# Two transformer layers on one core: the issue order of TensorE and the places of the small matrix products

## Chip, core and metric

The kernel runs on one core of a Trainium2 chip. Time is device microseconds of one launch; lower is better. TensorE (PE) multiplies matrices and transposes, VectorE (DVE), ScalarE (ACT) and GpSimd (POOL) work elementwise, SyncE (SP) issues the transfers.

## The reference

A sequence of 256 rows of 1024 numbers passes through two layers. Each adds a token mixer and then an MLP to the residual `x`. Layer 0 mixes with differential attention, layer 1 with sparse attention, in which an indexer chooses 64 keys for each query. The queries of a chunk of 64 rows see the keys of their own and of earlier chunks.

```python
for i in range(2):
    h = rms_norm(x, norm_mix[i])
    if i == 0:   # 8 heads, two softmaxes each
        q, k, v = split(h @ w_in)                  # q, k: 16 x 64, RMS-normed, rotary
        a = softmax(q1 @ k1.T) - lam * softmax(q2 @ k2.T)
        mix = (rms_norm(a @ v) * (1 - lam_init)) @ w_out
    else:        # 16 heads of 64
        c_q, k, v, k_idx, w_idx = split(h @ w_in)
        q, q_idx = rms_norm(c_q) @ w_uq, rms_norm(c_q) @ w_uq_idx
        score = sum_h(w_idx[h] * relu(q_idx[h] @ k_idx.T))
        chosen = top_k(score, 64)                  # per query
        mix = (softmax(q @ k[chosen].T) @ v[chosen]) @ w_out
    x = x + mix
    u = relu(rms_norm(x, norm_mlp[i]) @ w1)        # 1024 -> 4096
    x = x + (u * u) @ w2
```

All of it is float32. The indexer's choice is made as a mask here: all keys stay, and those not chosen get a large number added.

## The kernel before

**Wide products.** The weights come in units of 128 x 2048 numbers, 1 MB each (`unit`). A unit is split in two parts of reduced width whose sum is the number: ACT writes the high part (`whi`, L160), DVE the rest (`wlo`, L161, mostly in two pieces of 128 x 1024). The activations are kept in the same two parts. One wide product of the mathematics is three on PE (`mm3`, L164 to L170): high times high (L165), high times low (L167), low times high (L169), each 128 x 512 in the output. In the first half of an MLP it is two instructions (L492, L495). PE runs some 1,500 of these.

**Small products.** Between them stand the products of the mixers and the transposes:

- `make_h` (L242) transposes the residual into the next layer's input; ACT and DVE write the two parts (L246, L248). It is called for each half (256 columns) of a 128 x 512 block of the residual as soon as DVE has summed that half (L472 in `out_proj`, L542 in `mlp`).
- `qk_post` norms and rotates queries and keys on DVE (L381, L388, `rope` L366 to L369), and transposes them on PE, four transposes for each of two halves `b` (L398).
- `scores` multiplies queries and keys (`dots`, L414) and adds the mask while taking the minimum on DVE (L425); `expo` makes the exponentials on ACT (L436) after a small scale on DVE (L434).
- In layer 0, `diff_probs` mixes the two softmaxes of a head on DVE (L629). `to_keys` transposes the result (L443, three transposes), `weighted` (L450 to L452) multiplies by the values, and `diff_out` norms that and transposes it (L658) for the output projection.
- In layer 1, `compress` transposes the compressed queries (L718), `index` projects and rotates the indexer's queries and keys, transposes them (L754, L767), scores (L414) and chooses: eight rounds of a maximum and a replacement for each of two row blocks on DVE (L792, L793). `dsa_probs` makes the probabilities of 8 heads, normalised at L839, and `dsa_out` multiplies by the values (L850, L851).

**What sets the order.** The mixers' parts are Python generators. `spawn` runs one up to its first `yield`; `tick`, after each wide product of `mm3`, counts the waiting ones down and lets one go on when its count is at zero; `need` runs one to its end. The count comes from the table `PAUSE` by the name of the stage, and is 0 for a name that isn't in it; the table holds eight names. That sets the source's order. The engines' queues, PE's too, are then put in order by the framework's scheduler, which takes the instructions by its own estimate of when their operands are there; so PE's queue is not the source's order. Each engine runs its own queue in order. Waits between engines go through semaphores.

**Buffers.** Three raw units (`wraw`), four split units (`wsp`), four PSUM banks for wide products (`acc`) and four for small ones (`wk`), six score tiles (`s`).

Of the kernel before, what the change touches and what calls it, by code (L numbers as in the profile page):

```python
# [44 lines left out]
PAUSE = {"idx scores 1": 1, "idx transposes 0": 1, "idx transposes 1": 36, "q1 transposes 0": 1,  # L45
         "out0": 1, "out1": 2, "out2": 24, "out3": 27}
# [3 lines left out]
def trunk(ctx: ExitStack, tc: tile.TileContext, x_in, first_in, pack_in, wf, out):  # L50
# [59 lines left out]
    def pause(stage):  # L110
        return PAUSE.get(stage, 0)
# [123 lines left out]
    def make_h(h, gc, t, n, js=(0, 1)):  # L235

        hi, lo, _ = h[n]
        for j in js:
            ps = wk()[:, :256]
            for i in range(2):  # L240
                c = n * 4 + j * 2 + i
                nc.tensor.transpose(ps[:, i * 128:(i + 1) * 128], x[t][:, c * 128:(c + 1) * 128], ident)  # L242
            ops = [((slice(None), j * 2 + i, slice(t * 128, t * 128 + 128)), ps[:, i * 128:(i + 1) * 128],
                    pack[:, gc + n * 4 + j * 2 + i:gc + n * 4 + j * 2 + i + 1]) for i in range(2)]
            for o, p, g in ops:
                behind[:] = [nc.scalar.activation(hi[o], p, AF.Copy, scale=g).ins]  # L246
            for o, p, g in ops:
                nc.vector.scalar_tensor_tensor(lo[o], p, g, hi[o].bitcast(F32), op0=OP.mult, op1=OP.subtract)  # L248

    def lhs(h, kt, t):  # L250
        hi, lo = h[kt // 4][:2]
        c = slice(t * 128, t * 128 + 128)
        return hi[:, kt % 4, c], lo[:, kt % 4, c]
# [117 lines left out]
    def qk_post(ps, m, scon, ty, ng, nq, gcols, nm):  # L371
# [19 lines left out]
        res = []  # L391
        for b in range(2):
            yield pause(f"{nm} transposes {b}")
# [60 lines left out]
    def out_proj(o, us, h, gc, needs=((),) * 4):  # L454
# [3 lines left out]
        for u, (wh, wl) in enumerate(us):  # L458
# [3 lines left out]
            for n in range(2):  # L462
                for t in range(2):
# [5 lines left out]
                    if u == 3:  # L469
                        for j in range(2):  # L470
# [3 lines left out]
                            make_h(h, gc, t, n, (j,))  # L474

    def mlp(h, after):
# [4 lines left out]
        def up(b):  # L481
# [5 lines left out]
            def group(ps, m, ks):  # L487

                wh, wl = w[m // 2]
                c = slice((m % 2) * 128, (m % 2) * 128 + 128)  # L490
                for k in ks:
                    mm(ps.rearrange("p (a b) -> p a b", b=256), wh[:, k, c], h[k // 4][2][:, :, k % 4],  # L492
                       start=k == 0, stop=False)
                for k in ks:
                    mm(ps[:, 256:], wl[:, k, c], h[k // 4][0][:, k % 4], start=False, stop=k == 7)  # L495

# [24 lines left out]
        for b in range(NB):  # L521
# [9 lines left out]
            for t, u, n in order:  # L531
# [7 lines left out]
                if last and u == 1:  # L539
                    for j in range(2):  # L540
# [3 lines left out]
                        after(t, n, j)  # L544
# [66 lines left out]
    def diff_probs(ps, res, nm):  # L611
# [4 lines left out]
        sts = []  # L616
        for hh in range(2):
            yield pause(f"{nm} scores {hh}")
            sts.append(scores(qT, kT, hh, cmask))
        for hh in range(2):  # L620
            z, st = zs[:, hh], sts[hh]
# [9 lines left out]
            yield pause(f"{nm} keys {hh}")  # L631
            aTs.append(to_keys(a))
        res += [aTs, zs]

    def diff_out(j, aTs, zs):
# [18 lines left out]
        yield pause(f"out{j}")  # L654
# [28 lines left out]
    for n in range(2):  # L683
        v_part(n, h, srow)
        for j in (2 * n, 2 * n + 1):
            need(probs[j])
            outs.append(spawn(diff_out(j, *pr[j])))
# [3 lines left out]
    mlp(h, lambda t, n, j: make_h(h1, C_NORM + 16, t, n, (j,)))  # L691
# [19 lines left out]

    def compress():
        craw = sc.tile([128, 2, 328], F32, name="qn")
        pt = wk()
        for t in range(2):
            nc.scalar.activation(craw[:, t], cps[t][:, :328], AF.Copy)
# [8 lines left out]
        return craw  # L725

    def index(craw):
# [20 lines left out]
        yield pause("idx queries")  # L748
        ps = [wk() for _ in range(2)]
# [46 lines left out]
    craw = compress()  # L796
    chosen = spawn(index(craw))
# [12 lines left out]
    uq = [a.rearrange("p (k n) -> p k n", n=D) for a in unit(pieces=2)]  # L810
    for n in range(2):
# [10 lines left out]
    def dsa_probs(half, out):  # L822
# [4 lines left out]
        st = {}  # L827
        for p in range(5):
            yield pause(f"probs {half}{p}")
            if p < 4:  # L830
# [157 lines left out]
```

## Time and profile before

| | us |
|---|---|
| median of three runs (604.1 to 606.72) | 604.16 |
| the profiled execution | 605.11 |
| its span, first to last instruction | 602.9 |
| PE busy | 590.3 |
| DVE busy | 429.8 |
| ACT busy | 366.0 |
| mean granted clock of TensorE, share of full | 0.995 |

The span has these stages, by the times of the trace: the differential attention up to about 119 us, of which the projections with scores and mixtures lie at 24 to 64 and on to 90; the first MLP to about 290; the sparse attention from there to about 417, its index scores at 322 to 326, its first normal scores at 359; and the second MLP. PE's instructions are pipelined: a wide product is shown as 0.39 long, but the next one starts 0.23 behind it, so places are read from start to start. In a line of the timeline, x6 means that six alike instructions in a row stand together.

### The profile page before, as it was taken

What the parts mean: (1) busy time and instruction counts of PE and PEld (TensorE: products, weight loads), DVE (VectorE), ACT (ScalarE), POOL (GpSimd) and SP (SyncE); (2) the same over time, 40 slices, a digit from 0 to 9 for tenths busy, and PEclk for the clock granted to TensorE, in tenths of its full rate; (3) what the DMA queues carried; (4) which work ended last, traced back from release to release, by engine and by line L of the source; (5) the groups of instructions that cost most, each with busy time, mean ns of one, the idle gap of its engine ahead of it and who ended that gap; (6) DMA issues with size and microseconds to landing.
All of it is one profiled execution on the core that took longest, in us unless ns stands there. A gap on an engine that the chain in (4) does not pass through costs nothing.

```text
span 602.9 us, 8418 instructions
## 1 busy us (share of the span) xinstructions
PE 590.3 (98%) x3052; PEld 487.7 (81%) x3052; DVE 429.8 (71%) x1060; ACT 366.0 (61%) x711; POOL 18.8 (3%) x53
## 2 busy tenths in 40 slices
PE   9999999999999999999999899999999999999997
PEld 7777777888888888888787687768888888888885
DVE  6799975688656656657598999766886576567542
ACT  5998987575545545535497489785855355445420
POOL 6500000000000000000000000000000000000000
PEclk9999999999999999999999899999999999999999
DMA  8856334336555445545364226323475456456401
GB/s 312 334 205 221 133 139 141 140 140 223 204 201 204 170 186 209 195 161 188 140 210 140 71 70 219 131 79 132 151 268 198 160 201 210 162 188 209 140 1 70
DMA packets 15449, 103.35 MB, mean 171 GB/s; under 512 B 1712, under 2 KB 1968, under 8 KB 3760
## 3 DMA queue, kind: packets, MB, share of 16 engines
q1 hardware_dynamic: 15408, 102.82, 48.3%
q8 instruction: 24, 0.39, 0.2%
q14 instruction: 17, 0.14, 0.1%
HBM read 101.76 MB, written 1.05 MB: 171 GB/s over the span
## 4 chain that ended last, share of the span: by engine, by line
PE 83%; DVE 10%; ACT 3%; DMA 2%; issue 1%; SPq 0%; DVEq 0%; ACTq 0%
PE wk L492 18%; PE acc L167 16%; PE acc L169 15%; PE acc L165 15%; PE wk L495 9%; DVE wlo L161 3%; DVE s L425 2%; PE wk L443 2%; PE acc L492 1%; PE wk L414 1%; PE wk L242 1%; DMA raw<-in_first 1%; DMA raw<-in_w 1%; PE wk L398 1%; DVE qkss L381 1%
## 5 line engine op out<-in xcount | busy, mean ns | idle before, releaser
L161 DVE TENSOR_TENSOR wlo<-raw,whi 128x1024 fp32r<-128x1024 f32 (+2 forms) x206 | 225.3, 1124 | 107.0 <-ACT whi L160 106.5
L160 ACT ACTIVATE whi<-raw 128x1024 fp32r<-128x1024 f32 (+2 forms) x206 | 193.3, 979 | 87.8 <-issue 46.2
L167 PE MATMUL acc<-wlo,act 128*128 128x512 f32 (+1 forms) x504 | 198.7, 394 | 1.0 <-DVE wlo L161 0.8
L169 PE MATMUL acc<-whi,act 128*128 128x512 f32 (+1 forms) x504 | 198.5, 394 | 0.0
L165 PE MATMUL acc<-whi,act 128*128 128x512 f32 (+1 forms) x504 | 197.7, 394 | 0.0
L492 PE MATMUL wk<-act,whi 128*128 128x512 f32 x480 | 120.6, 392 | 0.0
L167 PEld LDWEIGHTS acc<-wlo,act 128*128 128x128 f32 x504 | 95.5, 190 | 21.3 <-DVE wlo L161 1.8
L169 PEld LDWEIGHTS acc<-whi,act 128*128 128x128 f32 x504 | 95.4, 189 | 19.5 <-issue 1.7
L165 PEld LDWEIGHTS acc<-whi,act 128*128 128x128 f32 x504 | 95.3, 190 | 18.3 <-issue 0.7
L492 PEld LDWEIGHTS wk<-act,whi 128*128 128x128 f32 x480 | 86.8, 189 | 15.8
L495 PEld LDWEIGHTS wk<-act,wlo 128*128 128x128 f32 x480 | 66.0, 190 | 5.1
L495 PE MATMUL wk<-act,wlo 128*128 128x256 f32 x480 | 67.5, 282 | 0.0
L503 ACT ACTIVATE act<-on 128x256 fp32r<-128x256 f32 x64 | 26.4, 416 | 52.0 <-DVE on L502 51.9
L436 ACT ACTIVATE s<-s,nb,rs_r 128x128 f32<-128x128 f32 x64 | 34.2, 537 | 8.7 <-DVE nb L434 8.7
L500 ACT ACTIVATE sq<-wk 128x256 f32<-128x256 f32 x60 | 22.4, 374 | 28.1 <-PE wk L495 28.1
L504 DVE TENSOR_TENSOR act<-on,act 128x256 fp32r<-128x256 f32 x64 | 26.9, 423 | 14.6 <-ACT act L503 13.0
L502 DVE SCALAR_TENSOR_TENSOR on<-sq 128x256 f32<-128x256 f32 x64 | 27.0, 424 | 1.7
L501 DVE TENSOR_TENSOR sq<-wk,sq 128x256 f32<-128x256 f32 x60 | 25.1, 419 | 0.1
L246 ACT ACTIVATE act<-wk,pack 128x128 fp32r<-128x128 f32 x48 | 13.8, 378 | 8.0 <-PE wk L242 8.0
L542 DVE SCALAR_TENSOR_TENSOR x<-acc,rows,x 128x256 f32<-128x256 f32 x16 | 7.0, 479 | 15.7 <-PE acc L169 15.7
L443 PE MATMUL wk<-pack,s 128*128 128x128 f32 x72 | 15.5, 286 | 2.7 <-DVE s L629 1.9
L443 PEld LDWEIGHTS wk<-pack,s 128*128 128x128 f32 x72 | 8.9, 140 | 10.4 <-DVE s L629 4.2
(185 smaller groups left out, 441.2 us busy)
## 6 DMA issues: line engine op xcount, KB each, us to landing
raw<-in_w SPq DMA_DIRECT2D x91, 1024.0 KB, 4.8
raw<-in_w SPq DMA_DIRECT2D x2, 512.0 KB, 8.3
x<-in_x SPq DMA_DIRECT2D x2, 512.0 KB, 6.5
raw<-in_w SPq DMA_DIRECT2D x1, 984.0 KB, 4.7
raw<-in_w SPq DMA_DIRECT2D x1, 840.0 KB, 4.6
raw<-in_first SPq DMA_DIRECT2D x1, 768.0 KB, 5.8
out_dram<-x SPq DMA_DIRECT2D x3, 256.0 KB, 2.0
raw<-in_first SPq DMA_DIRECT2D x1, 512.0 KB, 6.7
```

Of the source, the lines that this page charges most:

```text
L160: split[:] = [nc.scalar.activation(hi[:, c], raw[:, c], AF.Copy).ins]
L161: nc.vector.tensor_tensor(lo[:, c], raw[:, c], hi[:, c].bitcast(F32), op=OP.subtract)
L165: mm(ps, ah, wh, start=first, stop=False)
L167: mm(ps, ah, wl, start=False, stop=False)
L169: mm(ps, al, wh, start=False, stop=last)
L436: nc.scalar.activation(p[:, TS[t]], s[:, TS[t]], AF.Exp, bias=nb[:, t:t + 1], scale=nsc[:, t:t + 1], accum_out=z[t])
L443: nc.tensor.transpose(pt[:, i * 128:(i + 1) * 128], p[:, i * 128:(i + 1) * 128], ident)
L492: mm(ps.rearrange("p (a b) -> p a b", b=256), wh[:, k, c], h[k // 4][2][:, :, k % 4], start=k == 0, stop=False)
L495: mm(ps[:, 256:], wl[:, k, c], h[k // 4][0][:, k % 4], start=False, stop=k == 7)
L502: nc.vector.scalar_tensor_tensor(q, r, 0.0, r, op0=OP.max, op1=OP.mult)
L503: nc.scalar.activation(uh[:, m], q, AF.Copy)
L504: nc.vector.tensor_tensor(ul[:, m], q, uh[:, m].bitcast(F32), op=OP.subtract)
```

## The change

It does four things.

- PE's queue is taken out of the scheduler's hands: `tc.manual_schedule` for PE makes it issue in the order of the source. The other engines stay with the scheduler.
- `PAUSE` gets some forty names, so that each group of small products has a counted place among the wide ones; `tick` is also called in the first half of the MLP. `pause` takes several names and uses the first that is in the table.
- Groups are whole. `make_h` becomes a generator that makes all four transposes of a 128 x 512 block in one group, after both halves of the residual are written (a count of 5 wide products, 11 for one); whoever reads the block first calls `written`. The eight transposes of `qk_post` are one group. `diff_out` gets a count ahead of the products with the values.
- Some steps are cut differently: in `diff_probs` the exponentials and mixture of a head follow its own scores, ahead of the second head's; `compress` is a generator, with its copies from PSUM ahead of it; `dsa_probs` and `dsa_out` become one generator `dsa_half`, with scores two pairs ahead of the transposes.

The core of the diff, with a line or two of the table:

```diff
-PAUSE = {"idx scores 1": 1, "idx transposes 0": 1, "idx transposes 1": 36, "q1 transposes 0": 1,
-         "out0": 1, "out1": 2, "out2": 24, "out3": 27}
+PAUSE = {"a0 transposes": 68, "a3 transposes": 54, "transposes": 62, "scores 0": 11, "a3 scores 1": 14,
+         "keys 0": 28, "a3 keys 0": 12, "keys 1": 7, "a3 keys 1": 9,
...
-    def make_h(h, gc, t, n, js=(0, 1)):
+    later = {}
+
+    def make_h(h, gc, t, n, stage="h"):
+
+        def gen():
+            hi, lo, _ = h[n]
+            yield pause(stage)
+            ps = wk()
+            for i in range(4):
+                c = n * 4 + i
                 nc.tensor.transpose(ps[:, i * 128:(i + 1) * 128], x[t][:, c * 128:(c + 1) * 128], ident)
...
+        later[id(h), n, t] = spawn(gen())
+
+    def written(h, n, ts=(0, 1)):
+        need(*[later.pop((id(h), n, t)) for t in ts if (id(h), n, t) in later])
...
+        yield pause(f"{nm} transposes", "transposes")
         for b in range(2):
-            yield pause(f"{nm} transposes {b}")
             pt = wk()
...
         for hh in range(2):
-            yield pause(f"{nm} scores {hh}")
-            sts.append(scores(qT, kT, hh, cmask))
-        for hh in range(2):
-            z, st = zs[:, hh], sts[hh]
+            yield pause(f"{nm} scores {hh}", f"scores {hh}")
+            z, st = zs[:, hh], scores(qT, kT, hh, cmask)
...
-            yield pause(f"{nm} keys {hh}")
-            aTs.append(to_keys(a))
+            mixed.append(a)
+        for hh in range(2):
+            yield pause(f"{nm} keys {hh}", f"keys {hh}")
+            aTs.append(to_keys(mixed[hh]))
...
+        front(0)
+        front(1)
+        for p in range(4):
+            yield pause(f"{'second ' * half}half keys {p}", f"half keys {p}")
+            for e in ready.pop(p):
+                aTs.append(to_keys(e))
+            if p < 2:
+                front(p + 2)
...
     with tile.TileContext(nc) as tc:
-        trunk(tc, *args)
+        with tc.manual_schedule(engines={mybir.EngineType.PE}):
+            trunk(tc, *args)
```

The lines are numbered anew: L398 becomes L415 (transposes of queries and keys), L414 L431 (scores), L425 L442 (their reductions on DVE), L443 L460 (transposes of the mixture), L161 L169 (the split on DVE), L165/L167/L169 L173/L175/L177 (wide products), L629 L650 (the mixture on DVE).

What moves, at three places. The first is PE's queue in layer 0, where the first mixture of the first head pair is transposed. Before, twenty wide products behind the scores:

```order
L165 MATMUL acc<-whi,act 128x512
L443 MATMUL wk<-pack,s 128x128
L167 MATMUL acc<-wlo,act 128x512
L443 MATMUL wk<-pack,s 128x128 x2
L169 MATMUL acc<-whi,act 128x512
L165 MATMUL acc<-whi,act 128x512
L167 MATMUL acc<-wlo,act 128x512
L443 MATMUL wk<-pack,s 128x128
L169 MATMUL acc<-whi,act 128x512
L443 MATMUL wk<-pack,s 128x128 x2
L398 MATMUL wk<-pack,qn 128x128 x2
L165 MATMUL acc<-whi,act 128x512
```

After, twenty-eight behind them:

```order
L173 MATMUL acc<-whi,act 128x512
L175 MATMUL acc<-wlo,act 128x512
L460 MATMUL wk<-pack,s 128x128 x3
L177 MATMUL acc<-whi,act 128x512
L173 MATMUL acc<-whi,act 128x512
L175 MATMUL acc<-wlo,act 128x512
L415 MATMUL wk<-pack,qn 128x128 x8
L177 MATMUL acc<-whi,act 128x512
```

The three transposes of the first head stand together, the eight of the next pair's queries and keys too, and the second head's three come after these.

The second is DVE's queue at the same point, from the last score reduction of this pair to its mixture. Before:

```order
L425 ISA mn 128x1
L434 SCALAR_TENSOR_TENSOR nb<-mn,rs_r 128x2 x3
L190 SCALAR_TENSOR_TENSOR rs_a<-rs_a,rs_v 128x16
L192 TENSOR_TENSOR rs_y<-rs_y,scon_234 128x16
L161 TENSOR_TENSOR wlo<-raw,whi 128x1024
L624 RECIPROCAL rz<-zs 128x2
L193 SCALAR_TENSOR_TENSOR rs_r<-rs_a,rs_y 128x16
L161 TENSOR_TENSOR wlo<-raw,whi 128x1024
L626 SCALAR_TENSOR_TENSOR w<-zs,nlam,rz 128x2
L388 TENSOR_TENSOR qn<-qn,rs_r 128x256
L629 SCALAR_TENSOR_TENSOR s<-s,w 128x128
L629 SCALAR_TENSOR_TENSOR s<-s,w 128x256
```

After:

```order
L442 ISA mn 128x1
L451 SCALAR_TENSOR_TENSOR nb<-mn,rs_r 128x2
L169 TENSOR_TENSOR wlo<-raw,whi 128x1024
L451 SCALAR_TENSOR_TENSOR nb<-mn,rs_r 128x2
L645 RECIPROCAL rz<-zs 128x2
L169 TENSOR_TENSOR wlo<-raw,whi 128x1024
L647 SCALAR_TENSOR_TENSOR w<-zs,nlam,rz 128x2
L169 TENSOR_TENSOR wlo<-raw,whi 128x1024
L650 SCALAR_TENSOR_TENSOR s<-s,w 128x128
L650 SCALAR_TENSOR_TENSOR s<-s,w 128x256
```

Three splits stand between the scores and the mixture now, where two stood; and ahead of the scores, from the pair's last rope on, there are five (and the next pair's norm and rope) where there were three.

The third is PE's queue in layer 1, at the transposes of the second keys and of the first queries. Before, two and six of each, the queries' last six following in the same way:

```order
L398 MATMUL wk<-pack,qn 128x128 x2
L167 MATMUL acc<-wlo,act 128x512
L169 MATMUL acc<-whi,act 128x512
L165 MATMUL acc<-whi,act 128x512
L167 MATMUL acc<-wlo,act 128x512
L398 MATMUL wk<-pack,qn 128x128 x6
L169 MATMUL acc<-whi,act 128x512
L165 MATMUL acc<-whi,act 128x512
L167 MATMUL acc<-wlo,act 128x512
L398 MATMUL wk<-pack,qn 128x128 x2
```

After:

```order
L173 MATMUL acc<-whi,act 128x512
L415 MATMUL wk<-pack,qn 128x128 x8
L175 MATMUL acc<-wlo,act 128x512
L177 MATMUL acc<-whi,act 128x512
L173 MATMUL acc<-whi,act 128x512
L175 MATMUL acc<-wlo,act 128x512
L177 MATMUL acc<-whi,act 128x512
L173 MATMUL acc<-whi,act 128x512
L175 MATMUL acc<-wlo,act 128x512
L177 MATMUL acc<-whi,act 128x512
L173 MATMUL acc<-whi,act 128x512
L415 MATMUL wk<-pack,qn 128x128 x8
```

Both groups are whole, nine wide products apart, and stand six and eight products later than the first two transposes of each did.

## Rows read from the trace of the kernel before

**Rows 1.** The page: busy time, share of the span, instructions of each engine.

```profile
PE 590.3 (98%) x3052; PEld 487.7 (81%) x3052; DVE 429.8 (71%) x1060; ACT 366.0 (61%) x711; POOL 18.8 (3%) x53
```

**Rows 2.** Waits of PE: line, what it waited for; total, times, longest (us).

```profile
PE wk L398 <- DVE qn L369: 2.2, 1, 2.2
PE wk L443 <- DVE s L629: 1.9, 4, 0.6
...
PE wk L658 <- ACT on L653: 1.0, 1, 1.0
```

**Rows 3.** Windows: busy us (instructions) of PE, PEld, DVE, ACT, POOL; clock, DMA.

```profile
24.00:64.00 40.00, 38.62 (x202) 30.37 (x203) 38.51 (x131) 37.38 (x81) 2.83 (x6) 1.00 0.63 224
64.00:119.00 55.00, 52.96 (x288) 42.23 (x287) 38.84 (x132) 41.22 (x102) 0.00 (x0) 1.00 0.38 134
...
322.00:359.00 37.00, 34.82 (x175) 28.10 (x174) 35.16 (x130) 24.81 (x47) 0.00 (x0) 0.95 0.28 96
359.00:381.00 22.00, 21.41 (x115) 15.89 (x115) 21.71 (x86) 20.39 (x53) 0.00 (x0) 1.00 0.60 198
381.00:417.00 36.00, 35.38 (x219) 26.47 (x217) 22.21 (x83) 25.21 (x63) 0.00 (x0) 1.00 0.32 114
```

**Rows 4.** Timeline of PE at the first scores: start, length, instruction, [idle before].

```profile
33.71 0.82 PE L398 MATMUL wk<-pack,qn 128*128 128x128 f32 x6
...
36.31 1.58 PE L414 MATMUL wk<-qkT 64*128 64x128 f32 x16
...
42.51 0.39 PE L165 MATMUL acc<-whi,act 128*128 128x512 f32 x1
43.23 0.33 PE L443 MATMUL wk<-pack,s 128*128 128x128 f32 x1 [0.34 <-DVE s L629]
...
47.96 0.60 PE L398 MATMUL wk<-pack,qn 128*128 128x128 f32 x4
```

**Rows 5.** Timeline of DVE in the same stretch.

```profile
33.60 3.49 DVE L161 TENSOR_TENSOR wlo<-raw,whi 128x1024 fp32r<-128x1024 f32 x3
37.01 0.17 DVE L189 TENSOR_TENSOR rs_a<-rs_y 128x16 f32<-128x16 f32 x1
37.27 0.29 DVE L425 CUSTOM_DVE_ANT_0 s<-wk,cmask 128x128 f32<-128x128 f32 x1
...
39.78 0.17 DVE L190 SCALAR_TENSOR_TENSOR rs_a<-rs_a,rs_v 128x16 f32<-128x16 f32 x1
...
42.50 0.41 DVE L388 TENSOR_TENSOR qn<-qn,rs_r 128x256 f32<-128x256 f32 x1
42.84 0.74 DVE L629 SCALAR_TENSOR_TENSOR s<-s,w 128x128 f32<-128x128 f32 x2
...
43.57 0.27 DVE L366 TENSOR_TENSOR rp<-qn,rc 128x128 f32<-128x128 f32 x1
```

**Rows 6.** Timeline of PE in layer 1, at the transposes of the first keys.

```profile
341.40 0.66 PE L398 MATMUL wk<-pack,qn 128*128 128x128 f32 x2 [2.18 <-DVE qn L369]
...
342.28 0.63 PE L169 MATMUL acc<-whi,act 128*128 128x512 f32 x1
...
344.78 0.40 PE L169 MATMUL acc<-whi,act 128*128 128x512 f32 x1
```

**Rows 7.** Timeline of DVE at the end of the first output projection.

```profile
117.42 0.75 DVE L472 TENSOR_TENSOR x<-acc,x 128x256 f32<-128x256 f32 x2
118.08 0.68 DVE L161 TENSOR_TENSOR wlo<-raw,whi 128x512 fp32r<-128x512 f32 x1
```

**Rows 8.** Timeline of DVE in layer 1, where it waits itself.

```profile
322.95 0.69 DVE L381 TENSOR_REDUCE qkss<-sq 128x8 f32<-128x512 f32 x1 [0.59 <-ACT sq L380]
...
348.91 0.18 DVE L189 TENSOR_TENSOR rs_a<-rs_y 128x16 f32<-128x16 f32 x1 [0.31 <-ACT rs_y L188]
349.48 0.69 DVE L381 TENSOR_REDUCE qkss<-sq 128x8 f32<-128x512 f32 x1 [0.38 <-ACT sq L380]
...
358.56 1.28 DVE L381 TENSOR_REDUCE qkss<-sq 128x8 f32<-128x512 f32 x2 [0.16 <-ACT sq L380]
```

More of the change, by code (lines that the diff above doesn't have):

```diff
@@ L41 @@
             0.0014142135623842478, 0.00027424818836152554, 5.3182957344688475e-05, 1.0313385246263351e-05]
[L45 to L46 removed]
+PAUSE = {"a0 transposes": 68, "a3 transposes": 54, "transposes": 62, "scores 0": 11, "a3 scores 1": 14,
+         "keys 0": 28, "a3 keys 0": 12, "keys 1": 7, "a3 keys 1": 9,
+         "values 0": 8, "values 1": 12, "values 2": 8, "values 3": 12, "out": 30, "h": 5, "h last": 11,
+         "cq": 6, "idx queries": 14, "idx keys": 4, "idx transposes 0": 10, "idx transposes 1": 3,
+         "idx scores 0": 6, "idx scores 2": 8, "idx scores 3": 8,
+         "k0 transposes": 60, "k1 transposes": 49, "q0 transposes": 46, "q1 transposes": 90,
+         "heads 0": 39, "heads 1": 2, "half keys 0": 27, "half keys 1": 6, "half keys 2": 14, "half keys 3": 10,
+         "second half keys 0": 18, "second half keys 1": 7, "second half keys 2": 8, "second half keys 3": 8,
+         "sums": 4}
 @with_exitstack
@@ L107, in trunk, with pause @@
         mm(ps[:, :128], zero, zero, start=True, stop=True)
-    def pause(stage):
-        return PAUSE.get(stage, 0)
+    def pause(*names):
+        return next((PAUSE[n] for n in names if n in PAUSE), 0)
     side = []
@@ L748, in index @@
         yield pause("idx queries")
+        need(compressed)
         ps = [wk() for _ in range(2)]
@@ L810, in trunk @@
     uq = [a.rearrange("p (k n) -> p k n", n=D) for a in unit(pieces=2)]
+    need(compressed)
     for n in range(2):
@@ L820, in trunk, with dsa_half @@
     o = new_h()
-    def dsa_probs(half, out):
+    done, values = [], []
+    def dsa_half(half):
+        while half and not done:
+            yield 1
+        yield pause(f"heads {half}")
         need(chosen, posts[half], posts[2 + half])
@@ L856, in dsa_out, with store @@
         nc.vector.tensor_tensor(ol, ops, oh.bitcast(F32), op=OP.subtract)
+    halves = [spawn(dsa_half(half)) for half in range(2)]
     for half in range(2):
-        aTs = []
-        probs = spawn(dsa_probs(half, aTs))
         v_part(half, h, srow)
-        need(probs)
-        for i in range(2):
-            dsa_out(2 * half + i, aTs[4 * i:4 * i + 4])
+        values.append(half)
     h = new_h()
-    out_proj(o, take() + take(), h, C_NORM + 24)
-    def store(t, n, j):
-        if (t, n) != (1, 1) and j == 0:
-            return
-        c = slice(n * 512 + (j * 256 if (t, n) == (1, 1) else 0), n * 512 + j * 256 + 256)
+    out_proj(o, take() + take(), h, C_NORM + 24, [[halves[0]], [], [halves[1]], []])
+    def store(t, n, c):
         nc.sync.dma_start(out[t * 128:(t + 1) * 128, c], x[t][:, c])
```

88 lines of the change are left out of this document (49 added, 39 removed).

## Prediction

> **What bounds the kernel now.** I read four views, from coarse to fine. The page's busy times come first: TensorE (PE) is busy 590.3 of 602.9 us [rows 1], so only 12.6 us can come from waiting, and some 5 of them (1.0 at the start, 4.3 behind the last product) are not touched. The waits of PE say where the rest lies: one wait of 2.2 us of a q/k transpose for VectorE (DVE), four of L443, the transposes of the mixed probabilities, of 1.9 together, one of 1.0 for ScalarE (ACT) [rows 2]. The windows by stage then tell who is late. In both attention stages DVE has no air: 38.51 of 40 us at 24 to 64, 35.16 of 37 at 322 to 359, 21.71 of 22 at 359 to 381, while it is slack between the stages, 38.84 of 55 at 64 to 119 [rows 3]. So in these stages PE waits because a chain on DVE is late, and the small products are where it waits. The timelines show single places: the scores of the first head pair start at 36.31, wide products run at 0.2275 us from start to start until 42.51, and the first transposes of the mixture start at 43.23, 0.72 behind a product that needs 0.23 [rows 4]. The list has 0.34 of these 0.49; counted from start to start, the stage loses 5.2 us where the list has 2.9.
>
> [...]
>
> **What the change takes away.** Grouping as such is worth almost nothing: in the trace two transposes cost 0.23 us of PE and six 0.67, 0.11 each whatever the group, and 16 score instructions take 1.58 in their row, in one piece already [rows 4]. Over the 82 small groups I count 67.8 us from start to start, of which 52.7 are what the instructions need when nothing is late. [...] No transfer moves: SyncE's queue and GpSimd's are the same, and the splits of weights (L160, L161) keep their number. What moves is the places of the small products on PE, later by 4 to 15 wide products almost everywhere, and with them the order on DVE and ACT, which still is the scheduler's.
>
> **The first attention stage.** Nothing differs up to the three splits at 33.60. After that I add up DVE's queue in the order of the changed kernel, with the durations of the rows, up to the first mixture. It holds eight splits of 1.14 (three take 3.41 from start to start), 9.1 us, where the kernel before has five. Norm and rope of the next pair are ahead of the scores now: 0.34 and 0.67 for each of two tiles (a norm of 0.41; four rope operations, the first of 0.27; each overlaps the next by some 0.07), 2.0. Eight score reductions with their four small scales take 2.5 (37.27 to 39.78), four small operations 0.4, reciprocal, weight and the two mixing operations 0.9 [rows 5]. Sum 14.9, so the mixture is there at 33.60 + 14.9 = 48.5. PE gets there so: the last 2 of 8 transposes join the six at 33.71, wide products resume at about 35.0; eleven of them with a wait of 0.9 for the third split of that queue (37.1 against 36.2) bring it to 38.4; the scores take 1.6 to 1.7, the 28 products behind them 6.4, so 46.5 [rows 4]. It waits 2.0, where before it lost 0.5. The eight later products give PE 1.8 us to do, but the three splits now ahead of the mixture cost DVE 3.4. With these I get the transposes of the next pair 2 to 3 us later than before (second group at 47.96 [rows 4]).
>
> From there it comes back, since the splits done early are not wanted later: waits of 0.8 at the next mixture, none at the third, 1.05 at the output projection, 0.65 at the last keys, against 4.7 of before's 5.2. At the first transposes of the next h (117.89 before) I have **+1.0**; between −2 (DVE's operations in an order that fits) and +2.5 (nothing comes back).
>
> **The transposes into h**, at the ends of both output projections and of the first MLP. Each group of four now needs both halves of the residual sum, 0.75 for two, often with a split of 0.68 between them [rows 7], so 0.75 to 1.4 us, against five wide products (1.14) that cover it. A wait of nothing to 0.4 in each of the twelve groups, at most +2.7 by the order of DVE's queue at each; not below nothing, since L242 is not among PE's waits now. I take **+1.5**, nearer to the case with a split, because DVE's order puts one or two operations of the group before in between.
>
> **The sparse layer.** Two small waits are new: the index queries and the index keys each some 0.65, because two splits (2.3) stand ahead of the chain from the compressed row. Then from the index scores to the transposes of the first queries: PE has 117 wide products, 26.6 us, and 5.3 of small ones, 31.9; DVE has the index scores, the choice of keys, three norms and ropes and the splits, 36 by the rows, which agrees with 35.16 busy in that window before [rows 3]. So PE must wait 4.1 there, wherever the groups stand; before has 5.0 with its clock. DVE itself idles there now for 1.44 (0.59, 0.31, 0.38, 0.16) [rows 8], of which I leave it 1.3 more for PE to wait. One more wait of 1.8 comes at the third keys. That is 1.3 + 4.1 + 1.3 + 1.8 = 8.5 against 5.0 up to there. Behind it, before loses from 1.2 (PE's idle time in the windows 359 to 381 and 381 to 417 [rows 3]) to 3.4 us (start to start, six groups), the changed kernel about 1.5, since the choice of later places does help once DVE is slack. 8.5 + 1.5 − 5.0 − 3.4 = **+1.6**, between −2 and +4.
>
> **The clock.** Before pays 1.4 once; I count one such piece in the changed kernel too, so 0, and up to +2.8 if three waits of about 2 us do it. Whole groups of eight transposes do not lower the clock by the rows: 64 to 119 holds groups of six and of eight at a granted clock of 1.00 [rows 3]. [...]
>
> **Sum**: 1.0 + 1.5 + 1.6 + 0 = +4.1 us. The profiled execution took 605.11 (its span 602.9 and 2.2 around it), which gives 609.2; the median of the runs is 0.95 below that one, so 608.2.
>
> **Rivals.** *Later places remove the waits*: faster. Each group is asked for 4 to 15 products (0.9 to 3.4 us) later, longer than nearly every wait of the list. [...] It decides at the first mixture: if DVE has it before PE is through its 28 products, 46.5, the splits were not in its way, and the rest follows. Against it stand the windows, where DVE has 1.5 us of air in 40. *DVE binds and the sum stays*: the new waits are as long as those they replace, −3 to +3, 604. For it: the same operations on a full engine take the same time; the late first mixture and the h groups are against it. [...] That the change doesn't do what it says is no case: PE's order is fixed when the kernel is built.
>
> **Chances.** About 0.5% (3 us) is what a measurement of this kernel can tell from none. Forecast, 607.2 to 611: 0.39. Clock as well: 0.08. DVE binds, sum stays (601.1 to 607.2): 0.27. Waits removed (592 to 601): 0.26. So faster 0.26, same 0.27, slower 0.47. Both signs hold most of the chance: the forecast's own range is 605 to 612; the range of 8 in 10 goes from 596, half of the faster case left out below, to 613.
>
> **What would show it.** Right: a wait of L460 (the new line of the transposes of the mixture) on DVE of about 2 us at 46 to 49; DVE at 95% or more in 24 to 64; waits of L415 before the first sparse scores of 4 us or more together; the first MLP starting some 1 us later than before. Wrong: PE through that first mixture without a wait, or the two attention stages shorter than before by over 2 us; then the splits were done when I had them waiting, and my hand-made sum of DVE's queue is what failed. If the stages agree and the end is late, the h groups or the clock are mis-sized.

## The result: slower by 1.3%, twice the forecast

The changed kernel takes 612.47 us (median of four, 611.88 to 613.48), the kernel before 604.38; the ratio is 1.0127, 95% interval 1.0098 to 1.0156. The forecast was 608.2. The profiled execution has a span of 611.2 against 602.9, 8.3 us more.

The page of the changed kernel, to be read against [rows 1], and PE's waits against [rows 2] (line, what it waited for; total, times, longest):

```profile
PE 591.4 (97%) x3052; PEld 488.1 (80%) x3052; DVE 432.7 (71%) x1060; ACT 366.3 (60%) x711; POOL 18.5 (3%) x53
```

```profile
PE wk L415 <- DVE qn L386: 4.5, 3, 2.0
PE wk L460 <- DVE s L650: 3.2, 2, 2.9
...
PE wk L253 <- DVE x L489: 1.0, 4, 0.3
...
PE wk L253 <- DVE x L562: 0.6, 1, 0.6
```

PE's busy time has grown by 1.1 only; it waits more. The lines are those of before (L460 is the old L443, L415 the old L398), and L253, the transposes into h, is new on the list. Windows of the changed kernel, by the same stages as [rows 3] as far as they lie alike, and the two stretches at a lowered clock (the columns end with granted clock, DMA share, GB/s):

```profile
24.00:64.00 40.00, 36.69 (x183) 29.24 (x184) 36.71 (x124) 35.21 (x79) 2.54 (x6) 0.96 0.53 199
...
328.00:368.00 40.00, 35.52 (x179) 27.72 (x178) 37.70 (x138) 27.87 (x51) 0.00 (x0) 0.98 0.36 129
```

```profile
48.00:54.00 6.00, 5.18 (x23) 4.30 (x24) 4.90 (x15) 5.02 (x12) 0.00 (x0) 0.72 0.76 299
344.00:354.00 10.00, 10.00 (x49) 8.24 (x48) 9.90 (x35) 8.07 (x15) 0.00 (x0) 1.00 0.39 120
366.00:373.00 7.00, 6.99 (x36) 5.53 (x37) 6.02 (x34) 3.52 (x10) 0.00 (x0) 0.76 0.00 0
```

The first mixture, to be held against [rows 4] and [rows 5]. PE's timeline, then DVE's:

```profile
45.58 0.39 PE L175 MATMUL acc<-wlo,act 128*128 128x512 f32 x1
48.82 1.08 PE L460 MATMUL wk<-pack,s 128*128 128x128 f32 x3 [2.85 <-DVE s L650]
...
50.12 0.63 PE L173 MATMUL acc<-whi,act 128*128 128x512 f32 x1
50.55 0.63 PE L175 MATMUL acc<-wlo,act 128*128 128x512 f32 x1
```

```profile
44.42 1.21 DVE L169 TENSOR_TENSOR wlo<-raw,whi 128x1024 fp32r<-128x1024 f32 x1
...
46.03 1.21 DVE L169 TENSOR_TENSOR wlo<-raw,whi 128x1024 fp32r<-128x1024 f32 x1
...
47.28 1.22 DVE L169 TENSOR_TENSOR wlo<-raw,whi 128x1024 fp32r<-128x1024 f32 x1
48.42 0.74 DVE L650 SCALAR_TENSOR_TENSOR s<-s,w 128x128 f32<-128x128 f32 x2
```

PE stands still for 2.85 us behind three splits, and then runs its products 0.43 apart instead of 0.23; the granted clock is 0.50 from 48.8 to 52.

PE at the second keys and the first queries of the sparse layer, and at two of the four groups into h behind the first output projection, where the kernel before has no wait:

```profile
360.21 0.98 PE L415 MATMUL wk<-pack,qn 128*128 128x128 f32 x7 [2.03 <-DVE qn L386]
...
364.84 0.30 PE L415 MATMUL wk<-pack,qn 128*128 128x128 f32 x1 [1.57 <-DVE qn L386]
366.01 1.75 PE L415 MATMUL wk<-pack,qn 128*128 128x128 f32 x7 [0.87 <-DVE qn L386]
```

```profile
122.72 0.77 PE L253 MATMUL wk<-pack,x 128*128 128x128 f32 x4 [0.30 <-DVE x L489]
...
127.33 0.44 PE L253 MATMUL wk<-pack,x 128*128 128x128 f32 x2 [0.21 <-DVE x L489]
```

From start to start, three of these four groups lose 0.47, 0.25 and 0.37 us; the last two lose it between their second and third transpose, where the group goes on to the second half of the residual.

Where the time goes is best read from **the start of the same wide product** in two traces (the 160th product of one trace against the 160th of the other, worked out for this table). Later than before, in us, by profiled execution:

| wide product | place | changed kernel | scheduler orders PE |
|---|---|---|---|
| 154 | ahead of the first mixture | −1.5 | −1.5 |
| 160 | behind it | +3.7 | −0.4 |
| 370 | end of differential attention | +2.4 | −1.4 |
| 396 | first MLP running | +3.8 | −1.4 |
| 1320 | sparse layer begun | +5.3 | −1.6 |
| 1484 | ahead of second keys' transposes | +1.6 | −5.8 |
| 1500 | behind first queries' | +9.1 | −6.0 |
| 1637 | end of sparse attention | +7.1 | −3.9 |
| 1680 | second MLP running | +8.4 | −3.9 |

(Rows between two stages, 370, 396, 1320, 1637 and 1680, have the same small products ahead of them in all three traces. The others don't: −1.5 at 154 means no more than that small products come later there; 1484 stands behind the second keys' transposes in the kernel before and ahead of them in the other two, and at 1500 the first queries' transposes and the first scores are still to come where the scheduler orders PE.) So differential attention costs 2.4 us, the three places with transposes into h 1.4, 1.6 and 1.3, the sparse attention 1.7. The last column is the fourth experiment.

### The profile page after: what moved, and what is told of

It is laid out like the page before. It is cut to its first block, busy times and chain, and to the rows that moved or that the text cites. A ratio compares the mean times of both kernels' runs of the same rounds, so it can differ in the third digit from the quotient of the medians.

```text
span 611.2 us, 8429 instructions
## 1 busy us (share of the span) xinstructions
PE 591.4 (97%) x3052; PEld 488.1 (80%) x3052; DVE 432.7 (71%) x1060; ACT 366.3 (60%) x711; POOL 18.5 (3%) x53
## 3 DMA queue, kind: packets, MB, share of 16 engines
HBM read 101.76 MB, written 1.05 MB: 168 GB/s over the span
## 4 chain that ended last, share of the span: by engine, by line
PE 71%; ACT 12%; DVE 12%; DMA 4%; issue 1%; SPq 0%; DVEq 0%; ACTq 0%
PE wk L510 18%; PE acc L177 13%; PE acc L175 12%; PE acc L173 12%; PE wk L514 9%; DMA raw<-in_w 4%; ACT s L453 4%; DVE wlo L169 4%; ACT whi L168 3%; PE wk L431 1%; DVE act L260 1%; PE acc L510 1%; DVE score L823 1%; PE wk L253 1%; ACT qkT L418 1%
## 5 line engine op out<-in xcount | busy, mean ns | idle before, releaser
L169 DVE TENSOR_TENSOR wlo<-raw,whi 128x1024 fp32r<-128x1024 f32 (+2 forms) x206 | 225.3, 1124 | 106.7 <-ACT whi L168 106.7
L173 PE MATMUL acc<-whi,act 128*128 128x512 f32 (+1 forms) x504 | 198.0, 393 | 2.3 <-ACT act L904 1.0
L175 PE MATMUL acc<-wlo,act 128*128 128x512 f32 (+1 forms) x504 | 197.7, 392 | 1.3 <-DVE wlo L169 0.8
L177 PE MATMUL acc<-whi,act 128*128 128x512 f32 (+1 forms) x504 | 198.7, 394 | 0.2
L510 PE MATMUL wk<-act,whi 128*128 128x512 f32 x480 | 120.6, 392 | 0.0
L173 PEld LDWEIGHTS acc<-whi,act 128*128 128x128 f32 x504 | 95.1, 189 | 22.9 <-issue 1.7
L175 PEld LDWEIGHTS acc<-wlo,act 128*128 128x128 f32 x504 | 95.2, 189 | 22.0 <-issue 1.7
L177 PEld LDWEIGHTS acc<-whi,act 128*128 128x128 f32 x504 | 95.1, 189 | 20.2 <-issue 1.5
L510 PEld LDWEIGHTS wk<-act,whi 128*128 128x128 f32 x480 | 86.8, 189 | 15.8
L260 DVE SCALAR_TENSOR_TENSOR act<-wk,pack,act 128x128 fp32r<-128x128 f32 x48 | 14.3, 343 | 5.1 <-ACT act L258 5.0
L460 PE MATMUL wk<-pack,s 128*128 128x128 f32 x72 | 11.8, 283 | 3.5 <-DVE s L650 3.2
```

The lines of the kernel that those rows point to most:

```text
L169: nc.vector.tensor_tensor(lo[:, c], raw[:, c], hi[:, c].bitcast(F32), op=OP.subtract)
L173: mm(ps, ah, wh, start=first, stop=False)
L175: mm(ps, ah, wl, start=False, stop=False)
L177: mm(ps, al, wh, start=False, stop=last)
```

## The experiments

**One cost in the h groups: the tile.** In the changed kernel, where a group has one PSUM tile, ACT's second pair of copies waits for DVE's first pair (7.0 us in nine waits). A row of ACT in its trace:

```profile
122.37 0.63 ACT L258 ACTIVATE act<-wk,pack 128x128 fp32r<-128x128 f32 x2 [0.68 <-DVE act L260]
```

```diff
-            ps = wk()
+            two = [wk() for _ in range(2)]
```

> The changed kernel, but each group of four transposes into h has two PSUM tiles, two transposes in each, as the kernel before had; order and counts of the products stay. Theory 'chain': in one tile ACT's second pair of copies waits for DVE's first pair (0.68 us in the changed trace at each group), so a group takes four steps one behind the other and holds DVE's next residual sum; then the three places of the h groups, which cost 4.1 us more than before, cost some 2 less, and the time is 610.0 to 610.8. Rival 'both halves': the group waits for the whole block of the residual with too small a count, whatever the tiles; then the time stays at 612.5 within 0.6.

612.1 us, no gain. ACT's wait is gone, but PE now waits 3.5 us for the residual sums (1.6 before this edit): the place behind the first output projection costs 2.9 instead of 1.4, the one behind the MLP 0.4 instead of 1.6, the third 2.8 instead of 1.3.

**The count, and halves.** Two more tries at the same places:

```diff
-         ... "h": 5,
+         ... "h": 9,
```

> The changed kernel with a count of 9 instead of 5 wide products ahead of the h groups (11 stays for the last of the MLP). Theory 'too small a count for the whole residual': PE comes 0.9 us later to each group and the three places lose 1 to 1.5 instead of 4.1 us: 609.5 to 611. Rival 'the chain behind the group': what counts is when h is ready for the next stage's first products; later groups make that later and the place costs as much or more: 612 to 614.

612.35, as the rival said. PE no longer waits at the groups, but the first products of the next stage wait for h (L510 on DVE's L260, 2.7 us). In halves, at counts 3 and 6:

> The changed kernel with the h groups in halves of two transposes again, each with its own PSUM tile, the first at a count two below that of the changed kernel, the second three wide products behind the first; PE still in the order of the source. Theory 'both halves of the residual must be there for a whole group': the three places fall from 4.1 to 1 to 2 us more than before and the time is 610 to 611. Rival 'any counted place stops PE, whole group or half': 612 to 613.

612.82 (609.7 to 615.3); the places cost 1.4, 0.9 and 1.4. None of the three edits brings the 4 us back: neither the tile, nor the count, nor the whole group is by itself what has to be changed.

**The first mixture.** Twelve products later, and with one unit's low part left out:

```diff
-         "keys 0": 28,
+         "keys 0": 40,
```

> The changed kernel with 40 instead of 28 wide products between a head pair's first scores and the transposes of its first mixture in the first three pairs; DVE's queue up to that mixture is the same, with eight splits. Theory 'places too early for DVE': PE arrives 2.7 us later, the wait of 2.85 and the half clock behind it (1.4) go, and as DVE is full some of it comes back later; 609 to 611. Rival 'DVE's load alone sets the stage's end': the lag at the first h is the 2.4 us of the changed kernel again and the time 612.5 within 0.6. If keys so late collide with the next pair's scores, slower than 612.5.

609.48. The wait of 2.85 is gone, the granted clock in 24 to 64 is 1.00 (0.96 before the edit), product 160 starts 1.4 earlier than in the kernel before and product 370 1.0 earlier; the lag at the end is 3.7 where it was 8.4.

```diff
-            nc.vector.tensor_tensor(lo[:, c], raw[:, c], hi[:, c].bitcast(F32), op=OP.subtract)
+            if count[0] != LEFT_OUT:
+                nc.vector.tensor_tensor(lo[:, c], raw[:, c], hi[:, c].bitcast(F32), op=OP.subtract)
```

> The changed kernel without the low part of one weight unit (the fifth read after the first ones; GpSimd writes zeros there), so two splits less, 2.3 us of DVE, ahead of the first mixture; the output is not the reference's. Theory 'DVE's queue': the wait of 2.85 at the first mixture falls to 0.6 or less and the half clock behind it goes; at that place PE is 3 to 4 us ahead of the changed kernel, and at the first h 1.5 to 3; the time is 609.5 to 611. Rival 'ACT': ACT ends the exponentials late, the mixture waits for it and not for the splits; then the wait stays over 2 us and the time is 612 to 613.

609.96 (607.5 to 612.7; GpSimd writes zeros in the place of that low part), the wait 0.28. Both ways to meet the mixture work: PE later, or two splits of 1.14 fewer ahead of it on DVE. ACT is not it.

**Everything but the fixed order.**

```diff
-        with tc.manual_schedule(engines={mybir.EngineType.PE}):
-            trunk(tc, *args)
+        trunk(tc, *args)
```

> The changed kernel, all groups and counts as they are, but PE's queue is ordered by the scheduler again. Theory 'places': the scheduler takes the small groups by its estimate of when their operands are there, but h groups stay whole and in one tile; the attention stages go back to about the kernel before, the h groups keep some 3 of their 4 us: 606 to 609. Rival 'source order is not at fault': the counts decide also here, since the generators write the source in that order, and the time is 611 to 613.5.

**601.33 us**, faster than both kernels: ratio to before 0.9933 (95% interval 0.9912 to 0.9955). Neither theory had this. The new counts, the whole groups and the new cut of the steps are worth 0.7%; the fixed order takes 11 us away. Its trace at the two places (PE at the first mixture; DVE at the first residual sums, and the same place of the changed kernel):

```profile
47.37 0.33 PE L460 MATMUL wk<-pack,s 128*128 128x128 f32 x1 [0.34 <-DVE s L650]
...
47.77 0.44 PE L460 MATMUL wk<-pack,s 128*128 128x128 f32 x2
```

```profile
116.06 0.75 DVE L489 TENSOR_TENSOR x<-acc,x 128x256 f32<-128x256 f32 x2
116.72 0.68 DVE L169 TENSOR_TENSOR wlo<-raw,whi 128x512 fp32r<-128x512 f32 x1
117.32 0.75 DVE L489 TENSOR_TENSOR x<-acc,x 128x256 f32<-128x256 f32 x2
```

```profile
119.78 0.75 DVE L489 TENSOR_TENSOR x<-acc,x 128x256 f32<-128x256 f32 x2
120.45 1.28 DVE L169 TENSOR_TENSOR wlo<-raw,whi 128x512 fp32r<-128x512 f32 x2
121.72 0.61 DVE L260 SCALAR_TENSOR_TENSOR act<-wk,pack,act 128x128 fp32r<-128x128 f32 x2
122.25 0.75 DVE L489 TENSOR_TENSOR x<-acc,x 128x256 f32<-128x256 f32 x2
```

The scheduler put the mixture's transposes five wide products further back (behind the 160th, where the changed kernel has them behind the 155th); the wait there is 0.34. And at the residual DVE's own order differs: the next block's sum is 1.26 behind the first in this run, behind one half split; 2.47 in the changed kernel, behind two and two operations for h. From the first residual sum to the last low part of h DVE takes 8.8 us in the kernel before with one half split in between, 10.3 here with four, 11.5 in the changed kernel with six. PE loses nothing at this place in the run with 10.3, so the length of DVE's work alone isn't what costs.

**Is the sparse layer bound by DVE?** The transposes later, and less choice:

```diff
-         "k1 transposes": 49, "q0 transposes": 46,
+         "k1 transposes": 61, "q0 transposes": 60,
```

> The changed kernel with the transposes of the second keys 12 and of the first queries 14 wide products later (counts 61 and 60). Theory 'too early for DVE': the waits of L415 in layer 1 (2.0 and 2.0, with the half clock behind the second) go, PE does wide products there; 2 to 4 us less, 608.5 to 610.5. Rival 'DVE's load sets the time of the stage': the scores come when DVE is ready and the waits move to the next transposes or scores; at the end of the stage the lag is as in the changed kernel, 612 to 613, but for the clock (1.4).

```diff
-            for it in range(8):
+            for it in range(8 - 4 * t):
```

> The changed kernel with four instead of eight rounds of the choice of keys for the second row block (it keeps 32 keys there, so the output is not the reference's): some 3 us of DVE (0.74 each round) less ahead of the transposes of the second keys and first queries. Theory 'DVE is the bound of this stretch': PE's waits there fall by 3 and the half clock behind them goes, 608 to 610. Rival 'the chain of norm and rope, or ACT': these waits stay within 0.6 and the time 612 to 613.

Later transposes give nothing: 613.61 (610.5 to 614.6), and product 1637 lags by 7.0 as before the edit (7.1). PE's waits at L415 fall from 4.5 to 3.1, but the clock is lower there (0.51 in 366 to 373, 0.76 before the edit), so this run alone doesn't tell the two theories apart. Three us less of DVE's work give 3.4 at product 1637 (lag 3.6): PE's waits at L415 fall from 4.5 to 2.2, and behind the first queries' transposes, where the changed kernel's wide products stand 0.43 apart from 368.0 on, they stand 0.23 apart (from 364.5 on). That profile is of the fastest of four runs; their median is 610.99, above the 608 to 610 that was expected, but below the changed kernel. From DVE's first index score to its first reduction of sparse scores it takes 38.2 us in the kernel before, 40.2 in the changed one, 39.1 with the later transposes, 37.4 with less choice, 37.1 where the scheduler orders PE. DVE idles 2.2 of it in the changed kernel, 1.3 with either edit, 0.1 where the scheduler orders PE. So DVE's queue sets most of this stretch, and moving PE's transposes of keys and queries didn't help. But the places on PE cost here as well: of the 3.1 us between the changed kernel and the scheduler's order 2.1 are DVE's own idle time, 1.1 around the index scores, which stand in three pieces, and 1.0 at the end, where it waits for the first scores:

```profile
370.62 0.29 DVE L442 CUSTOM_DVE_ANT_0 s<-wk,smask 128x128 f32<-128x128 f32 x1 [0.98 <-PE wk L431]
```

**Other priorities on DVE, PE's queue unchanged.**

```diff
+        with tc.high_priority():
```

It stands around norm and rope, the mixture, and the residual sums.

> The changed kernel with PE's queue exactly as it is, but with a higher priority in the scheduler for three pieces of DVE's work: norm and rope of queries and keys, the mixture of a head, and the residual sums of the output projections. In DVE's queue the residual sums now stand ahead of two splits, and norm and rope of the second keys and first queries ahead of most rounds of the choice of keys; at the first mixture the same eight splits stay ahead. Theory 'DVE's order': most of the loss against the order of the scheduler (601.3) is that DVE does other things first than PE's fixed order wants; the output projections' h groups then fall from 1.4 to under 0.7 each, the waits at the second keys and first queries from 4 to under 2, the first mixture keeps its 2.9 and the half clock: 606.5 to 609.5. Rival 'PE's fixed order': with PE in a row nothing can pass a late group, whatever DVE does; 611 to 613.5.

> The same priorities and, as in the run with the later first mixture (609.5), 40 wide products ahead of the transposes of the first mixtures; PE in the order of the source. Theory 'DVE's order and a few places': both repairs add up, 3 from the mixture and 3 to 5 from the priorities: 602.5 to 606.5, within 0.5% of the kernel before. Rival 'fixed order': the one repair alone, 608.5 to 610.5.

> The same priorities with PE's queue left to the scheduler. Theory 'DVE's order': without the fixed order DVE's queue already fits (601.3 in that run), so little is left to gain: 599.5 to 602. Rival: the priorities take the choice of keys out of its place and it comes late for the first sparse scores: 602 to 605.

616.01, 611.14 and 604.66 (603.3 to 608.4): worse each time than the same kernel without the priorities, by 3.5, 1.7 and 3.3; only the third rival had its range right. The waits only move: the first residual sums are earlier, and the MLP waits for h (2.5); the second keys are earlier, and the first sparse mixtures wait (L461, 3.4). The fixed order costs 11.3 in this pair of kernels too (616.01 against 604.66).

**One engine's queue held in the other kernel's order.** Edges that fix only the order of issue, made behind the last line of the kernel:

```diff
+        for a, b in zip(ranks, ranks[1:]):
+            tc.add_manual_dep(mine[b], mine[a].name,
...
+                              reason="given order")
```

> The changed kernel with PE's queue exactly as it is (order of the source), but DVE's queue held in the order that it has in the run without the fixed order (601.3); ACT is left to the scheduler. Theory 'DVE's queue': what costs 11 us between the two is the order in which DVE works, which the scheduler plans differently once PE is fixed; 602 to 606. Rival 'PE's queue': with PE in the order of the source a late group stops all wide products behind it, whatever DVE's order is; 608 to 613.

> The other half: PE's queue held in the order of the run without the fixed order, DVE's and ACT's queues held in the order that they have in the changed kernel. Theory 'DVE's queue': 608 to 612. Rival 'PE's queue': 601 to 605. If both this run and the other one come out in the middle, the two orders only fit each other, and the loss belongs to the pair.

618.52 and 609.78. With PE fixed, DVE's order from the faster run is worse than its own by 6.0; with the faster run's PE order, DVE's and ACT's orders from the changed kernel cost 8.5. The second alone would speak for 'DVE's queue', the first is outside both ranges. In these two pairs an order was good only with the other engines' orders that it was planned with, so neither PE's nor DVE's order alone holds the loss.

**Splits on GpSimd.**

```diff
-            nc.vector.tensor_tensor(lo[:, c], raw[:, c], hi[:, c].bitcast(F32), op=OP.subtract)
+            (nc.gpsimd if i in pool else nc.vector).tensor_tensor(lo[:, c], raw[:, c], ...)
```

> The changed kernel with 24 of the splits of the attention stages (the second half of each unit of a pair, 1.14 us of DVE each) on GpSimd, which is idle there; PE in the order of the source, the same counts. Theory 'DVE's load is the clock of both attention stages': DVE has 27 us less to do, the waits at the first mixture, the second keys and first queries shrink by more than half; 600 to 607. Rival 'GpSimd is too slow or gets in DVE's way': splits late for the wide products or DVE's operations longer than in the rows; 612 or more.

> The same 24 splits on GpSimd with PE's queue left to the scheduler. Theory 'DVE's load': below the 601.3 of that kernel, 595 to 600. Rival 'GpSimd is too slow or in the way': 601 to 606.

639.26 and 634.01. A split took GpSimd 2.5 us, and in the second of these runs twenty operations of DVE took 39 us longer than in the changed kernel (last section), so this says nothing on DVE's load.

**Which places.** Here the same edges hold PE's queue in the faster run's order, without `manual_schedule`. The changed kernel's PE queue differs from that order in 27 short stretches, 3 to 68 instructions each. Three groups of these (1, 7 and 10 stretches) are put back as in the source, one group at a time, with DVE and ACT planned anew; the other nine, all in layer 0, were not put back by themselves. Of the list of places in the queue the first are shown:

```diff
+ORDERS = {"PE": "0+10 12 10+2 13+3 18 16+2
...
+    impose(tc, nc)
...
-        with tc.manual_schedule(engines={mybir.EngineType.PE}):
-            trunk(tc, *args)
+        trunk(tc, *args)
```

> PE's queue held in the order of the run without the fixed order (601.3; held so, all queues are line for line that run's), but for one place, which is as in the changed kernel: the three transposes of the first mixture come three wide products earlier and in one piece, the eight of the next pair three products behind them. DVE and ACT are planned anew. Theory 'a few places': the first mixture is waited for 2 to 3 us again with the half clock behind it, and the time is 603.5 to 605.5. Rival 'the loss is spread': within 0.7 of 601.3.

> The same, but only the transposes into h (end of both output projections, end of the first MLP) stand as in the changed kernel, whole and at the counts. Theory 'a few places': the three places cost the 4 us that they cost in the changed kernel, 604.5 to 606. Rival: DVE's and ACT's plan there comes from elsewhere, under 602.5.

> The same, but only the sparse layer's stretch, from the compressed row to the last products with the values, stands as in the changed kernel. Theory 'a few places': the second keys' and first queries' transposes wait 2 and 2 to 4 us again with the half clock, and as DVE's load sets this stage a good part of it comes back by its end; 603.5 to 606. If the three runs sum to some 11 over 601.3 the loss is a sum of places; if they sum to much less, it is the whole plan.

603.49, 608.96 and 605.39: 2.2, 7.6 and 4.1 more than 601.33, in sum 13.9 where all together cost 11.1. So the places of the groups bring the loss back, without `manual_schedule`; they don't add, and what the nine others are worth isn't known. Holding the order costs next to nothing by itself: DVE's and ACT's queues are the faster run's, line for line, up to 315 us in the third run and from 90 us on in the first, and the third run's lag is 0.4 up to there. (In the first of these runs the mixture's transposes stand five wide products earlier than in the faster run, not three as expected above.) The largest is h. Lags against the faster run, by the starts of wide products (the third run's profiled execution was 2.7 above its median):

| wide product | changed | first mixture | h | sparse layer |
|---|---|---|---|---|
| 160 | 4.1 | 0.8 | −0.7 | 0.4 |
| 370 | 3.7 | 1.8 | −0.7 | 0.5 |
| 396 | 5.1 | 1.8 | 0.8 | 0.4 |
| 1320 | 6.9 | 1.8 | 2.6 | 0.4 |
| 1484 | 7.4 | 1.8 | 2.9 | 2.0 |
| 1500 | 15.0 | 1.8 | 7.8 | 9.4 |
| 1637 | 10.9 | 1.8 | 6.1 | 6.9 |
| 1680 | 12.2 | 1.8 | 7.5 | 6.9 |

At 1500 the changed kernel and the sparse run have eight transposes and sixteen scores, some 2.5 us, ahead of the product that come later in the faster run; the rows at 1637 and 1680 are free of this. The h run loses 1.4, 1.8 and 1.3 at its three places, and 3.6 more in the sparse layer, where PE's order is the faster run's and only DVE's and ACT's plans have changed: nine splits instead of seven stand ahead of the first sparse reduction, 40.6 us after the first index score instead of 37.1. PE there:

```profile
355.46 0.41 PE L417 MATMUL wk<-pack,qn 128*128 128x128 f32 x2 [1.90 <-DVE qn L388]
358.41 1.54 PE L417 MATMUL wk<-pack,qn 128*128 128x128 f32 x6 [1.84 <-DVE qn L388]
```

## Where the prediction was right and where it failed

The sign, the mechanism and the first place held: groups at counted places wait for DVE, first at the first mixture. The size did not: +4.1 by the sum, +8.4 measured at product 1680. Of the 4.3 that are missing, 2.8 are the transposes into h and 1.4 the first attention stage.

- **The transposes into h: +1.5 in the sum, +4.3 measured. This is the step that failed.** The wait for both halves of the residual came as written, and at the first place three of four groups lose 0.25 to 0.47 from start to start, near the 0.4 that the working allowed. But by its own words a wait of up to 0.4 in each of twelve groups is up to 4.8, and the bound was set at 2.7, the value at 1.5, an eighth of a us for each group; it is 0.36 (4.3 over twelve). DVE's order there, two lines of [rows 7], was taken as one split between sums; it is two and two operations for h. The same groups, alone in the source's order, cost 1.4, 1.8 and 1.3 as well, and 3.6 more by the plans of DVE and ACT in the sparse layer, which the sum has no term for.
- **First attention stage: +1.0 in the sum, +2.4 measured.** The waits that the working lists (0.9 and 2.0, then 0.8, 1.05 and 0.65) come to 5.4 against 5.2 before, so +0.2 and not +1.0. The mixture was put at 48.5, its transposes start at 48.82, with the eight splits ahead of it that the change shows. PE was there earlier than the 46.5 of the sum, as the wait of 0.9 for a split didn't come, so the wait is 2.85 and not 2.0. What is missing beside this is the clock behind that wait (0.50 from 48.8 to 52). That losses come back later held: the lag falls from 3.7 to 2.4, with waits of 0.74 and 0.33 behind the first mixture.
- **The clock: 0 in the sum, some +1.7**, an estimate from the granted clock (0.28 of the 6 us below), which lies within the stages' figures above and below. It counted one stretch as before; there are two, within 48 to 54 (0.72) and 366 to 373 (0.76). No row shows the 1.4 that it counts for a stretch: by [rows 6] six products lose 1.1 together, at a granted clock of 0.52 in 342.28 to 344.78, and the other 0.3 was an estimate. In the changed kernel the clock is 0.50 from 48.8 to 52 and 0.57 from 366 to 370. That whole groups lower it, the trace doesn't show: the window 344 to 354 holds a group of eight for which nothing waits, at 1.00, and the group at 360.21 stands behind 2.03 us of waiting, with the clock at 1.00 from 360 to 364 too; it fell at 366.0, behind two more waits (1.57 and 0.87). (In the kernel before, the longest row of transposes in 64 to 119 has six, and not eight as the prediction reads it; one of eight stands at 381.7, in a window at 1.00 [rows 3].)
- **The sparse layer: +1.6 in the sum, +1.7 measured, in part by luck.** The waits at the second keys and first queries were put at 5.4 (4.1 and 1.3) and come to 4.5, with the clock at 0.76 in 366 to 373 beside them (some 1.7 us, 0.24 of the 7). But the index queries and keys wait 0.7 and not 1.3, and the 1.8 at the third keys doesn't come: from 366.1 to 393 PE has no wait over 0.12. The reading behind it held: DVE's load decides, as the run with less choice shows.
- **What would have shown it**: the waits of L460 and L415 came as written; the transposes into the first MLP's h start 2.4 and the MLP runs 3.8 later, not 1; DVE is not at 95% but at 92% in 24 to 64 (36.71 of 40): the longest of its new waits, 1.07 at 53.75, is for ACT, which had itself waited 0.90 for PE's late transposes.
- **The rivals.** 'Later places remove the waits' was turned down for the kernel as a whole, and its deciding point, the first mixture by 46.5, went against it. But with the same counts and groups the kernel is faster, 601.3, once the scheduler may order PE's queue. I weighed the order of PE's queue only as a fact of the change, never as one of its parts with a price. The 'clock as well' case, at a chance of 0.08 the one above the forecast's 611, holds the time, by another sum: one more stretch (0.72 in 48 to 54), and h.

What stays open: why the scheduler's plan for DVE puts more splits ahead once PE's places are as in the source. That it does is in the rows; no run here changed its estimates. The three h edits under the fixed order gave nothing, and the loss there was not undone other than by leaving PE to the scheduler.

## What to carry to other kernels

When an instruction order is fixed on one engine while others are still planned, its places and their plans must fit each other. A group that is five products too early stopped PE for 2.85 us here, and the groups into h, put back alone, changed the order on DVE and ACT in the sparse layer behind them, where that cost 3.6 us more. Leave out the fixing alone before judging the rest: here the rest was a gain of 0.7% and the fixing a loss of 1.9%. And where an engine is full for a whole stretch, take its work away: here moving PE's transposes that wait for it gave nothing, and three us less of its work gave 3.4 at the end of the stage in one profile and 1.5 in the median.

## What the runs showed of the hardware

DVE stood still beside splits on GpSimd. In the run with splits on GpSimd and PE ordered by the scheduler, an operation of 128 x 16 on DVE that takes 0.16 in the changed kernel takes 2.33, until GpSimd's split that began just ahead of it ends (DVE, then GpSimd):

```profile
41.77 2.33 DVE L201 SCALAR_TENSOR_TENSOR rs_r<-rs_a,rs_y 128x16 f32<-128x16 f32 x1
```

```profile
41.66 2.40 POOL L169 TENSOR_TENSOR wlo<-raw,whi 128x1024 fp32r<-128x1024 f32 x1 [0.33 <-ACT whi L168]
```

What holds DVE there no run shows. The split takes GpSimd 2.5 us (mean of 24) and DVE 1.14 from start to start. In this run twenty operations of DVE are longer than their like in the changed kernel, by 39 us together (worked out from the two traces), where the 24 splits would have taken DVE 27; so DVE lost more time by the move than it was spared.

The clock was not lowered behind every wait: in the run with only the first mixture put back PE waits 1.82 there, and the window behind it has a clock of 1.00. Nor did the longer wait always have the lower clock. At that mixture PE waits 2.71 in the run with later sparse transposes and the clock is 1.00 from 48 to 54; it waits 2.40 in the run with less choice, with the same order on PE and DVE up to there, and the clock is 0.72 (2.85 and 0.72 in the changed kernel's profile). What decides it no run here shows.

```profile
46.00:51.00 5.00, 4.14 (x25) 3.42 (x26) 4.56 (x14) 5.00 (x11) 0.00 (x0) 1.00 0.55 213
```
